# Two more feature tiles of one feed-forward half by seven half-size products, and more low parts made by adding DMAs

## The chip, the cores and the metric

One core of a Trainium2 chip runs the whole program. The metric is device microseconds of one execution, the median of the runs shown; a profiled execution is taken beside them. Engines are named as the profile names them: PE does the matrix products, ACT and DVE the elementwise work, POOL the small powers and the issue of DMAs that add, SP the issue of loads.

## The reference, cut to what matters

Two layers over 256 context and 256 latent tokens of width 1024. Each layer is a feed-forward half, a token mixer, and a second feed-forward half:

```
def swiglu(x, w_in, w_out):
    gate, up = jnp.split(x @ w_in, 2, axis=-1)
    return (jax.nn.silu(gate) * up) @ w_out

h  = h  + 0.5 * g1  * swiglu(modulate(rms_norm(h,  norm), sh1,  sc1),  ffn1_w_in, ffn1_w_out)
hc = hc + 0.5 * cg1 * swiglu(modulate(rms_norm(hc, norm), csh1, csc1), ffn1_w_in, ffn1_w_out)
# ... mixer, then the same again with norm_ffn2, sh2, sc2, g2, ffn2_w_in, ffn2_w_out
```

`w_in` is 1024 x 5632 (2816 gate and 2816 up columns), `w_out` 2816 x 1024. Context and latent tokens go through the same weights. The shifts, scales and gates come from a product of `silu(c)` with a 1024 x 9216 matrix in each layer.

## The kernel before, in words

Activations lie transposed in SBUF, 128 features by 512 tokens (256 context, 256 latent) a tile. Every operand of a large product is split in two: a high part, rounded to the matrix engine's format (`whi`, `xh`, `hh`), and a low part that holds the remainder (`wlo`, `xl`, `hl`). A product is three matmuls: high with high, high weight with low activation, low weight with high activation (`mm3`, L825 to L827).

**Four feed-forward halves.** They are named (layer, half): (0,1), (0,2), (1,1), (1,2). The 2816 features are 22 tiles of 128, in groups (`GROUPS`): in (0,2) tiles 0 to 7, 8 to 14 and 15 to 21. For a group, PE first makes the gate and up products of each tile, then contracts the group's tiles with `w_out` into the eight output tiles. A plain tile takes 16 blocks of three 512-column matmuls.

**Seven products.** From tile `DIRECT[l, half]` on, a tile is made in another way: gate and up, the two token halves and the two halves of the 1024 inputs are taken as a 2 x 2 block product, which seven products of half the size give instead of eight (`fast`, `fasts`). Each of the seven is four blocks of three 256-column matmuls, 84 matmuls a tile. The factors are sums of weight blocks and sums of activations. `seven(c)` (L711) makes the weight factors of a tile out of its two raw chunks of 512 KB: A, B, C of 1024 columns each in slots of a ring of six, and D of 512 columns in a pool of its own. Each has a high part made on ACT (`hi`, L729) and a low part made on DVE (`lo`, L723). The order of the products of tile f on PE is fixed in `fasts`: 1, 5, then product 3 of the tile before, 6, 2, product 4 of the tile before, 7. Product 2 is the first that reads B:

```
P7 = {1: ("A", 0, "X", ["A11"]), 6: ("C", 1, "X", ["C"]), ..., 2: ("B", 1, "Y", ["B"])}
for n in (1, 5, -3, 6, 2, -4, 7):
```

The opening of ring slots is a chain through the steps' waits: C of tile f waits for B of f-1, A of f+1 for C of f, B of f for A of f+1. A product that is the last to read a factor gives the slot back: 5 gives back A, 7 C, 4 B.

**Low parts by DMA.** Where `SEVENTH` (for A and B of seven-product tiles) or `SOFT` (for plain chunks) says so, the low part is not made on DVE. ACT writes the negated high part into it (`negate`, L360 for a plain chunk, L772 for A or B), and a DMA issued from POOL adds the raw weights out of HBM onto it (`add_raw`, L366; `add`, L777). Which tiles are taken follows from the fraction; for B:

```
n = SEVENTH[u, l, ww]
return int((f + 1) * n) > int(f * n)
...
if soft7("b"):
    yield S("ACT", act(1024), lambda: negate("B", whole, raw(1, whole)), give={"raw": 1}, wait=[ev("s4")])
    yield S("SW", 2.7, lambda: add("B", c + 1, whole), fire=ev("B"), lag=3.0)
```

**What sets the order.** All steps are generators with a priority (`Step`, `Weave`). At build time a planner goes through them with modelled costs and writes one fixed order of instructions for each engine; of the steps that can start within 0.12 us of each other on an engine it takes the most urgent. A smaller number is more urgent. `URG` holds four of the priorities, among weights at 18 (`U_W`), evacuation of plain tiles at 12 and the modulation products at 90. On the chip each engine runs its list in order and waits on semaphores.

**Modulation products.** The shifts, scales and gates of later stages are made on DVE (`gemv`, L882, two of 1.2 us for each of the 48, 48 and 24 jobs of the halves (0,1), (0,2), (1,1)), each after a 512 KB load. `pump` lets a number of jobs in after each plain tile, each output tile and each seven-product tile: the three numbers of `RATES` for a half. `to_mixer` (L2161) holds the next stage back until all of them are done.

**Stages in the trace.** (0,1) runs to about 395 us, the first mixer to about 600, (0,2) to 986, (1,1) to about 1330, the second mixer to about 1512, (1,2) to the end. The mixer's last output tiles overlap the first part of the half behind it.

Of the kernel before, what the change touches and what calls it, by code (L numbers as in the profile page):

```python
# [29 lines left out]
KT = 8  # L30
NF = FF // 128
GROUPS = {(0, 1): (0, 8, 15, 22), (0, 2): (0, 8, 15, 22), (1, 1): (0, 8, 15, 22), (1, 2): (0, 11, 22)}
DIRECT = {(0, 1): 13, (0, 2): 10, (1, 1): 4, (1, 2): 22}
EPS = 1e-6
CH = 8
LAT = slice(256, 512)
# [18 lines left out]
def groups(l, w):  # L55

    g = GROUPS[l, w]
    return [range(a, b) for a, b in zip(g, g[1:])]


def plan():
# [3 lines left out]
    def ffn(l, w):  # L65
# [3 lines left out]
        for fs in groups(l, w):  # L69
            for f in fs:  # L70
                if f >= DIRECT[l, w]:
                    out.extend(((kind, l, w, f), CH) for kind in ("sa", "sb"))
# [319 lines left out]
class Weave:  # L392
# [62 lines left out]
    def run(self):  # L455
# [37 lines left out]

SLACK = {"PE": 0.12, "ACT": 0.12, "DVE": 0.12, "POOL": 0.0, "DMA": 0.0, "SW": 0.0}
U_W, U_MAIN, U_EVAC, U_GEMV = 18, 50, 12, 90
URG = {'seven': 17.3, 'evac7': -5.8, 'sums': (50.8, 54.3, 50.1), 'last': 3.6}
RATES = ((8.61, 1.92, 8.82), (2.29, 5.11, 4.25), (0.59, 2.29, 1.25))
N_POOL, N_VECTOR = 6, 12
SEVENTH = {('b', 0, 1): 0, ('a', 0, 1): 0, ('b', 0, 2): 0, ('a', 0, 2): 1, ('b', 1, 1): 0, ('a', 1, 1): 0}
SOFT = {('fi', 0, 1): 0,  # L500
        ('fo', 0, 1): 0,
        ('fi', 0, 2): 0,
        ('fo', 0, 2): 0,
        ('fi', 1, 1): 0.8,
# [44 lines left out]
def emit(tc, xT, cc, wmod, wst, cols_d, cst_d, nab, gates, wm0, ccol, out, layers=L):  # L549
# [3 lines left out]
    with es:  # L553
# [25 lines left out]
        def ot():  # L579
            return op_.tile([128, 512], F32, name="o")  # L580
# [3 lines left out]
        def S(*a, **k):  # L584
            return Step(*a, **k)

        def act(n, ap=0):
            return 0.1 + 0.00083 * n + (0.0, 0.05, 0.19)[ap]
# [8 lines left out]
        def dve(n):  # L597
            return 0.06 + 0.00105 * n
# [12 lines left out]
        def half(s):  # L611
            return slice(s * 256, (s + 1) * 256)
# [98 lines left out]
        def seven(c):  # L711
# [7 lines left out]
            def raw(i, h):  # L719
                return g["ab"[i]][:, h]  # L720

            def tt(o, x0, x1, op):
                V.tensor_tensor(o, x0, x1, op)  # L723

            def ev(*e):
                return ("s7", l, ww, f) + e
# [7 lines left out]
            run = next(r for r in groups(l, ww) if f in r)  # L734
            begins, ends = f == max(run[0], DIRECT[l, ww]), f == run[-1]
            whole = slice(0, 1024)
# [4 lines left out]
            def first():  # L741
# [13 lines left out]
                if soft7("a"):  # L755
                    yield S("ACT", act(512), lambda: negate("A", a, raw(0, a)), fire=ev("nA"))
                    w.spawn(URG["seven"], a11(), w.at[ev("nA")])
                else:
# [3 lines left out]
                yield S("DVE", dve(512), lambda: tt(g["x"][:, b], raw(0, b), raw(0, a), OP.subtract), fire=ev("s2"))  # L762
                w.spawn(URG["seven"], third(), w.at[ev("s2")])
                w.spawn(URG["seven"], fourth(), w.at[ev("s2")])

            def soft7(u):

                n = SEVENTH[u, l, ww]
                return int((f + 1) * n) > int(f * n)

            def negate(u, h, src):
                A.activation(g[u][1][:, h], src, AF.Copy, scale=-1.0)  # L772
# [6 lines left out]
            def a11():  # L779
                yield S("SW", 1.4, lambda: add("A", c, a), fire=ev("A11"), lag=3.0)  # L780

            def third():
                def open_c():
                    g["C"] = W.unit()
                    hi("C", whole, g["x"])
                yield S("ACT", act(1024), open_c, take={"ring": 1}, wait=[] if begins else [other(-1, "openB")],
                        fire=ev("openC"))
                yield S("DVE", dve(1024), lambda: lo("C", whole, g["x"]), wait=[ev("s4")], give={"sx": 1},
                        fire=ev("C"))
# [11 lines left out]
            def second():  # L801
# [7 lines left out]
                if soft7("b"):  # L809
# [5 lines left out]
                        fire=ev("B"))  # L815
            w.spawn(URG["seven"], first())
            w.spawn(URG["seven"], second())

# [24 lines left out]
        def open_ffn():  # L843
            st, ph["start"] = ph["st"], _ = ExitStack(), ExitStack()
            which = ((0, 1), (0, 2), (1, 1), (1, 2))[ph.get("n", 0)]
            GF, some = max(map(len, groups(*which))), DIRECT[which] < NF
            ng = 2 if some else 6
# [183 lines left out]
        def ffn(l, ww, p, streams, nxt, rates, start):  # L1031
# [63 lines left out]

            us = dict(zip(((0, 1), (0, 2), (1, 1)), URG["sums"])).get((l, ww))

# [69 lines left out]
            def seeded():  # L1167

                def go():
                    u = S7[l, ww, DIRECT[l, ww]]["A"][0]  # L1170
                    yb.append(ot())
                    PE.matmul(yb[0][:, qa], u[:, :128], XH[:, KT - 1, half(0)], start=True, stop=True)
                yield S("PE", 0.11, go, take={"o": 1}, give={"o": 1}, wait=[("s7", l, ww, DIRECT[l, ww], "openA")])

# [33 lines left out]
            def fasts(f, run):  # L1208
                prev = f - 1 if f > max(run[0], DIRECT[l, ww]) else None
                for n in (1, 5, -3, 6, 2, -4, 7):  # L1210
# [954 lines left out]
        def main():  # L2165
            want(0, (2, 4, 3, 5, 7, 6))
            open_ffn()
            startup()
            yield from ffn(0, 1, 0, (0, 1), (0, 3), RATES[0], True)
            yield from to_mixer()  # L2170
# [3 lines left out]
            open_ffn()  # L2174
            yield from ffn(0, 2, 2, (0, 1), (1, 0), RATES[1], False)
            yield from to_mixer()
            want(1, (5, 7, 6))
            open_ffn()
            yield from ffn(1, 1, 3, (0, 1), (1, 3), RATES[2], False)
            yield from to_mixer()  # L2180
# [34 lines left out]
```

## Time and profile before

| | |
|---|---|
| median of 3 runs | 1701.85 us (1701.08 to 1703.96) |
| profiled execution, its own time | 1702.62 us |
| its span | 1700.8 us |
| PE busy | 1673.5 us, 98% |
| DVE busy | 1380.7 us, 81% |
| ACT busy | 880.4 us, 52% |
| POOL busy | 168.6 us, 10% |
| mean granted clock of PE | 0.997 |

The span runs from the first to the last instruction that the profiler saw; the time of the execution is 1.8 us more. A busy PE is not PE at its peak, since matmuls overlap: the distance between the starts of two matmuls tells its pace.

### The profile page before, as it was taken

To read this page: it belongs to the slowest core of one execution; us is meant where nothing else is said; L and a number is where in the kernel's file an instruction comes from. 1 tells how busy PE (TensorE), PEld (TensorE's weight loads), DVE (VectorE), ACT (ScalarE), POOL (GpSimd) and SP (SyncE) were. 2 spreads that over 40 slices of the span, in tenths; PEclk is the share of its full clock that TensorE was granted. 3 is DMA by queue.
4 is the path that set the end of the run, shared out by engine and by line. 5 is a ranking of instruction groups with operands and counts; after the bars stand their busy time and mean duration, and the time that the engine had idled before them with its cause. 6 is when DMAs were issued, how large, how long until landed. Compare 5 with 4: busy or idle time off the path is not lost.

```text
span 1700.8 us, 28038 instructions
## 1 busy us (share of the span) xinstructions
PE 1673.5 (98%) x10843; PEld 1455.8 (86%) x10843; DVE 1380.7 (81%) x2349; ACT 880.4 (52%) x1507; POOL 168.6 (10%) x157
## 2 busy tenths in 40 slices
PE   7999999999999999999999999999999999999999
PEld 4688888989767688888989899899898977699999
DVE  6987898997778779888989879588597878889664
ACT  4433244544768544234546465456455477765342
POOL 1201001011111110010010110200201212010000
PEclk9999999999999999999999999999999999999999
DMA  8558658373211124695786753955837323166552
GB/s 304 183 160 248 207 171 221 119 221 98 89 60 56 51 86 151 222 254 141 222 207 179 217 135 116 257 158 176 218 125 235 108 84 96 65 229 240 180 183 95
DMA packets 85273, 279.23 MB, mean 164 GB/s; under 512 B 10386, under 2 KB 13714, under 8 KB 84756
## 3 DMA queue, kind: packets, MB, share of 16 engines
q1 hardware_dynamic: 73620, 251.23, 44.8%
q0 software_dynamic: 11520, 26.22, 8.7%
q8 instruction: 85, 1.39, 0.3%
q14 instruction: 48, 0.39, 0.1%
HBM read 263.78 MB, written 1.05 MB: 156 GB/s over the span
## 4 chain that ended last, share of the span: by engine, by line
PE 88%; DVE 7%; ACT 2%; issue 2%; DMA 0%; SPq 0%; POOL 0%; POOLq 0%; ACTq 0%; DVEq 0%
PE mm L825 18%; PE mm L827 18%; PE mm L826 18%; PE mm L1193 4%; PE mm L1195 4%; PE mm L1194 4%; PE tr L1194 2%; PE tr L1193 2%; PE tr L1195 2%; PE sc L1704 1%; PE o L1757 1%; PE o L1195 1%; PE o L1194 1%; PE o L1193 1%; PE tr L1680 1%
## 5 line engine op out<-in xcount | busy, mean ns | idle before, releaser
L825 PE MATMUL mm<-xh,whi 128*128 128x512 f32 (+2 forms) x1098 | 380.8, 347 | 3.1 <-ACT xh L975 1.9
L826 PE MATMUL mm<-xl,whi 128*128 128x512 f32 (+2 forms) x1098 | 365.9, 333 | 3.8 <-DVE xl L976 2.7
L827 PE MATMUL mm<-xh,wlo 128*128 128x512 f32 (+2 forms) x1098 | 365.0, 332 | 0.0
L349 ACT CAST whi<-wraw 128x1024 fp32r<-128x1024 f32 (+1 forms) x238 | 248.4, 1044 | 212.3 <-PE mm L826 173.1
L882 DVE SCALAR_TENSOR_TENSOR junk<-graw,silc 128x1024 f32<-128x1024 f32 x256 | 315.9, 1234 | 24.9 <-DMA graw<-in_wmod_dram 22.3
L355 DVE TENSOR_TENSOR wlo<-wraw,whi 128x1024 fp32r<-128x1024 f32 (+2 forms) x213 | 260.2, 1223 | 69.0 <-ACT whi L349 67.5
L827 PE MATMUL mm<-hh,wlo 128*128 128x512 f32 (+1 forms) x724 | 260.8, 360 | 0.0
L826 PE MATMUL mm<-hl,whi 128*128 128x512 f32 (+1 forms) x724 | 258.5, 357 | 0.0
L825 PE MATMUL mm<-hh,whi 128*128 128x512 f32 (+1 forms) x724 | 258.4, 357 | 0.0
L825 PEld LDWEIGHTS mm<-xh,whi 128*128 128x128 f32 x1098 | 208.0, 189 | 35.2 <-issue 10.3
L826 PEld LDWEIGHTS mm<-xl,whi 128*128 128x128 f32 x1098 | 208.4, 190 | 30.0 <-issue 5.3
L827 PEld LDWEIGHTS mm<-xh,wlo 128*128 128x128 f32 x1098 | 208.0, 189 | 22.2 <-DVE wlo L355 0.4
L826 PEld LDWEIGHTS mm<-hl,whi 128*128 128x128 f32 x724 | 136.1, 188 | 23.4
L825 PEld LDWEIGHTS mm<-hh,whi 128*128 128x128 f32 x724 | 136.1, 188 | 21.5
L827 PEld LDWEIGHTS mm<-hh,wlo 128*128 128x128 f32 x724 | 136.0, 188 | 21.3
L723 DVE TENSOR_TENSOR wlo<-wraw,whi 128x512 fp32r<-128x512 f32 (+1 forms) x105 | 92.4, 886 | 35.6 <-ACT whi L729 35.2
L729 ACT CAST whi<-wraw 128x512 fp32r<-128x512 f32 (+1 forms) x117 | 88.9, 763 | 49.9 <-PE mm L826 32.1
L1024 ACT ACTIVATE h<-mm,mod 128x256 f32<-128x256 f32 x96 | 40.4, 472 | 128.2 <-PE mm L827 93.8
L1195 PE MATMUL mm<-t7h,wlo 128*128 128x256 f32 x312 | 88.1, 282 | 0.0
L1194 PE MATMUL mm<-t7l,whi 128*128 128x256 f32 x312 | 87.9, 282 | 0.0
L1028 POOL DMA_DIRECT2D x<-h x48 | 41.9, 873 | 463.3 <-ACT h L1024 358.1
L1193 PE MATMUL mm<-t7h,whi 128*128 128x256 f32 x312 | 87.7, 281 | 0.0
(312 smaller groups left out, 3530.8 us busy)
## 6 DMA issues: line engine op xcount, KB each, us to landing
wraw<-in_wst_dram SPq DMA_DIRECT2D x308, 512.0 KB, 3.7
graw<-in_wmod_dram SPq DMA_DIRECT2D x137, 512.0 KB, 4.6
x<-h POOLq DMA_DIRECT2D x48, 256.0 KB, 5.7
wlo<-in_wst_dram POOLq DMA_DIRECT2D x20, 512.0 KB, 9.1
graw<-in_wm_dram SPq DMA_DIRECT2D x7, 512.0 KB, 7.1
silc<-in_cc_dram SPq DMA_DIRECT2D x3, 1024.0 KB, 7.0
wlo<-in_wst_dram POOLq DMA_DIRECT2D x12, 256.0 KB, 4.5
x<-in_xT_dram SPq DMA_DIRECT2D x8, 256.0 KB, 4.3
```

Of the source, the lines that this page charges most:

```text
L349: self.nc.scalar.copy(hi[:, :n], self.raws[i][:, :n])
L355: eng.tensor_tensor(lo[:, :n], self.raws.pop(i)[:, :n], hi[:, :n].bitcast(F32), OP.subtract)
L723: V.tensor_tensor(o, x0, x1, op)
L729: A.copy(g[u][0][:, h], src)
L825: PE.matmul(o, wh[:, :m], h, start=start, stop=False)
L826: PE.matmul(o, wh[:, :m], lo, start=False, stop=False)
L827: PE.matmul(o, wl[:, :m], h, start=False, stop=stop)
L882: V.scalar_tensor_tensor(ph["junk"], g["r"], 1.0, ph["sc"][:, s, :], OP.mult, OP.mult, accum_out=mod[l, c][:, s, j:j + 1])
L1028: yield S("SW", 1.4, lambda: G.dma_start(x[:, dt, :], g["t"], accum_op=OP.add), lag=3.0, give={"h": 1})
L1193: PE.matmul(o, wh, xh, start=n in (1, 5) and k == 0, stop=False, **on)
L1194: PE.matmul(o, wh, xl, start=False, stop=False, **on)
L1195: PE.matmul(o, wl, xh, start=False, stop=k == 3, **on)
```

## The change

Numbers that the planner reads are changed, and no function. `DIRECT` of (0,2) goes from 10 to 8, so tiles 8 to 21, 14 of them, are made by seven products, where 10 to 21 were. Of the low parts of A in (0,2) half are made by adding DMAs, where all were; of B 0.34, where none were. In (0,1) half of the low parts of A and a quarter of the plain `w_out` chunks (from chunk 12 on) are made by adding DMAs, where none were. `URG` and `RATES` get other values.

```
-DIRECT = {(0, 1): 13, (0, 2): 10, (1, 1): 4, (1, 2): 22}
+DIRECT = {(0, 1): 13, (0, 2): 8, (1, 1): 4, (1, 2): 22}
...
-URG = {'seven': 17.3, 'evac7': -5.8, 'sums': (50.8, 54.3, 50.1), 'last': 3.6}
-RATES = ((8.61, 1.92, 8.82), (2.29, 5.11, 4.25), (0.59, 2.29, 1.25))
+URG = {'seven': 14, 'evac7': -6.6, 'sums': (39.8, 22.4, 49.5), 'last': 3.6}
+RATES = ((2.5, 0.61, 32.34), (19.02, 20.23, 51.94), (0.3, 2.64, 5.69))
...
-SEVENTH = {('b', 0, 1): 0, ('a', 0, 1): 0, ('b', 0, 2): 0, ('a', 0, 2): 1, ('b', 1, 1): 0, ('a', 1, 1): 0}
+SEVENTH = {('b', 0, 1): 0,
+           ('a', 0, 1): 0.5,
+           ('b', 0, 2): 0.34,
+           ('a', 0, 2): 0.5,
+           ('b', 1, 1): 0,
+           ('a', 1, 1): 0}
 SOFT = {('fi', 0, 1): 0,
-        ('fo', 0, 1): 0,
+        ('fo', 0, 1): 0.25,
         ('fi', 0, 2): 0,
```

## Rows read from the trace of the kernel before

**Rows 1.** The page, part 1: busy time (share of the span) and instructions.

```profile
PE 1673.5 (98%) x10843; PEld 1455.8 (86%) x10843; DVE 1380.7 (81%) x2349; ACT 880.4 (52%) x1507; POOL 168.6 (10%) x157
```

**Rows 2.** Stretches: length, busy us of PE, PEld, DVE, ACT, POOL; PEclk, DMA share, GB/s.

```profile
66.00:395.00 329.00, 329.00 (x1810) 283.32 (x1810) 294.59 (x473) 137.20 (x224) 22.65 (x21) 1.00 0.64 191
645.00:986.00 341.00, 341.00 (x2033) 301.12 (x2032) 298.70 (x472) 159.19 (x267) 33.73 (x37) 1.00 0.69 200
```

**Rows 3.** Timeline of PE: start, us, line, operation; tile 8 begins, seven products begin.

```profile
764.67 0.39 PE L825 MATMUL mm<-xh,whi 128*128 128x512 f32 x1
...
787.15 0.28 PE L1172 MATMUL o<-xh,whi 128*128 128x256 f32 x1
```

**Rows 4.** Timeline of PE: product 2 of tiles 16, 17; between, product 1 of 17.

```profile
889.52 0.28 PE L1195 MATMUL o<-xh,wlo 128*128 128x256 f32 x1
...
893.54 0.28 PE L1193 MATMUL mm<-xh,whi 128*128 128x256 f32 x1
...
899.40 0.28 PE L1195 MATMUL o<-xh,wlo 128*128 128x256 f32 x1
```

**Rows 5.** Timeline of ACT: high part of B of tile 17, [idle before <-releaser].

```profile
892.18 1.05 ACT L729 CAST whi<-wraw 128x1024 fp32r<-128x1024 f32 x1 [0.91 <-PE mm L1194]
893.14 0.61 ACT L1235 CAST hh<-h 128x512 fp32r<-128x512 f32 x1
```

**Rows 6.** Timelines of ACT and POOL: one negation and its 512 KB adding DMA.

```profile
963.63 1.06 ACT L360 ACTIVATE wlo<-wraw 128x1024 fp32r<-128x1024 f32 x1
...
965.09 0.88 POOL L366 DMA_DIRECT2D wlo<-in_wst_dram  x1 [0.73 <-ACT wlo L360]
```

**Rows 7.** Line L366, 512 KB adds: all 20, then the three of 960:980.

```profile
DMA to landing us min/median/max: 7.0/9.1/12.3
...
DMA to landing us min/median/max: 7.0/7.0/7.7
```

**Rows 8.** Line L777, 256 KB adds of A: the four of 880:925.

```profile
DMA to landing us min/median/max: 4.0/4.1/6.8
```

**Rows 9.** Stretches, columns as in rows 2.

```profile
880.00:925.00 45.00, 45.00 (x384) 45.00 (x383) 43.09 (x74) 29.37 (x55) 3.48 (x4) 1.00 0.62 162
1062.00:1074.00 12.00, 12.00 (x97) 11.72 (x96) 10.10 (x19) 6.86 (x12) 1.73 (x2) 1.00 0.95 269
```

**Rows 10.** Two neighbouring stretches of the start, columns as in rows 2.

```profile
55.00:58.40 3.40, 0.80 (x4) 0.21 (x2) 3.40 (x7) 2.04 (x4) 0.70 (x1) 0.99 0.66 235
58.40:61.60 3.20, 3.20 (x8) 2.52 (x9) 3.13 (x5) 0.83 (x2) 0.00 (x0) 0.50 0.05 19
```

**Rows 11.** DVE groups in 645:986: shapes, count, busy us, mean ns, idle before.

```profile
L355 DVE TENSOR_TENSOR wlo<-wraw,whi 128x1024 fp32r<-128x1024 f32 x36 | 44.5, 1237 | 7.2 <-ACT whi L349 7.1
L723 DVE TENSOR_TENSOR sx<-wraw 128x512 f32<-128x512 f32 x24 | 16.5, 688 | 0.3
...
L1231 DVE TENSOR_TENSOR h<-sg,h 128x256 f32<-128x256 f32 x12 | 5.0, 420 | 0.4 <-ACT sg L1228 0.4
```

**Rows 12.** Timelines: end of the last modulation job; first product of (1,1).

```profile
970.03 0.17 DVE L896 TENSOR_TENSOR mod<-mod,cols 128x16 f32<-128x16 f32 x1
...
986.06 0.28 PE L825 MATMUL mm<-xh,whi 128*128 128x256 f32 x1
```

**Rows 13.** Timelines: B's high part and product 2 of tiles 14 and 15.

```profile
820.57 1.05 ACT L729 CAST whi<-wraw 128x1024 fp32r<-128x1024 f32 x1
...
830.34 0.28 PE L1195 MATMUL o<-xh,wlo 128*128 128x256 f32 x1
...
865.17 1.05 ACT L729 CAST whi<-wraw 128x1024 fp32r<-128x1024 f32 x1 [1.87 <-PE mm L826]
...
880.97 0.28 PE L1195 MATMUL o<-xh,wlo 128*128 128x256 f32 x1
```

**Rows 14.** Timelines: first output chunk of (0,1)'s last group, cast and first use.

```profile
344.86 1.05 ACT L349 CAST whi<-wraw 128x1024 fp32r<-128x1024 f32 x1 [0.40 <-PE mm L1194]
...
359.40 0.40 PE L827 MATMUL mm<-hh,wlo 128*128 128x512 f32 x1
```

## The prediction

> **What bounds the kernel.** I read the page's busy shares first, then the table of stretches, then the timelines of PE, ACT, DVE and POOL around the seven-product tiles of (0,2), and last the adding DMAs by line. PE is busy 98% of the span [rows 1], and in the two stretches that the change touches, 66 to 395 us for (0,1) and 645 to 986 us for (0,2), it is busy for the whole length at a granted clock of 1.00 [rows 2]. The pace agrees: between the start of tile 8 and the start of the seven products lie two plain tiles, 96 matmuls in 787.15 - 764.67 = 22.48 us, 0.234 us each with no gap [rows 3]. So in (0,1) and (0,2) the time is PE's column count, and nothing that only relieves DVE or ACT shortens it. DVE is the next: 298.7 of 341 us in (0,2) and 294.6 of 329 us in (0,1) [rows 2]. A gain must come out of fewer matmul columns, and a loss out of any factor that reaches PE late.
>
> **Two tiles fewer by the plain way.** A plain tile costs 22.48 / 2 = 11.24 us [rows 3]. A seven-product tile in the steady part of a group costs the distance of product 2 of tile 16 to product 2 of tile 17, 899.40 - 889.52 = 9.88 us [rows 4]. Two tiles change kind: 2 x (9.88 - 11.24) = -2.7 us. They are tiles 8 and 9, so that group two becomes like group three, all seven tiles of one kind; group three runs without a gap today, so I charge no new seam.
>
> **DVE's part of it.** A plain tile has two subtractions of 1024 and two of 512 columns, 2 x 1.24 + 2 x 0.69 = 3.9 us. A seven-product tile has two of 1024, eight of 512 (one of them A's low part) and four of 256: 2.5 + 5.5 + 1.7 = 9.7 us [rows 11]. Two tiles add 11.6 us. Twelve A parts went by DMA and seven will: +3.4 us. Five B parts leave DVE: 5 x 1.24 = -6.2 us. Net +8.8 us in a stretch that has 42 us of idle DVE, mostly in slivers. What gives way are the modulation jobs, the least urgent work. The last one ends at 970.2 us, and PE needs it at 986.06, when (1,1) begins [rows 12]: 15.9 us of cover, less the 2.7 us that PE gains. If all 8.8 us came out one for one as delay, 4.4 us would be left. I charge 0; with that cover gone each further microsecond of DVE is one of PE.
>
> **B's low part by DMA.** The rule with 0.34 takes tiles 8, 11, 14, 17 and 20. Tile 17 stands in the trace. B's high part is cast at 892.18, after ACT had waited 0.91 us for PE to give a ring slot back, and ends at 893.23 [rows 5]. The first matmul that reads B's low part starts at 899.40 [rows 4]. That leaves 6.2 us, and the lead can't grow with earlier work, because the slot, not ACT or DVE, sets it: the six openings of two tiles lie between B of tile 15 and B of tile 17, and B of 15 is given back by product 4, one product (1.4 us) before tile 17 begins. Today DVE fills the gap with 1.2 us of work. In its place come: the cast of `hh`, more urgent, to 893.75 [rows 5]; the negation, 1.06 us; 0.40 us from its end to the start of the DMA on POOL (964.69 to 965.09) [rows 6]; and the landing of a 512 KB adding DMA. For the landing the nearest rows are the 20 of line L366, 7.0 to 12.3 us with a median of 9.1 [rows 7], and the 256 KB adds of A in this very stretch, 4.0 to 6.8 us [rows 8]. The stretch moves data in 0.62 of its time, against 0.95 where the pair of slowest adds was under way [rows 9], and the three adds in 960 to 980 took 7.0 to 7.7 us [rows 7]. I take 7.0: the low part is there at 893.75 + 1.06 + 0.40 + 7.0 = 902.2 us, 2.8 us late. PE's list has nothing to put in the gap, since the order of the products is fixed and in-order. Bounds: with 4.1 us it is on time (0), with 12.3 us it is 8.1 us late.
>
> Tiles 11, 17 and 20 are of this steady kind: third, fourth or sixth in their groups. Each stall stands for itself, because the next lead is again counted from PE's own release: 3 x 2.8 = 8.4 us. Tile 14 is last in its group and has more: its cast ends at 821.62 and product 2 needs the low part at 830.34, 8.7 us, against 1.06 + 0.40 + 7.0 = 8.5: 0 (with 9.1 us 1.9 late). Tile 8 will open its group as tile 15 does now, with 880.97 - 866.22 = 14.7 us [rows 13]: 0 at any landing in the rows.
>
> The Trainium skill has a rule that speaks against this stall: "DMA: Bandwidth & Descriptors", section "Anatomy of one DMA", fits a DMA issued from POOL with 2.0 us plus its bytes over 436 GB/s. For 512 KB that is an estimate of 3.2 us; by it the low part of tile 17 would be there at 898.4 us, before PE wants it, and the sum would be -2.7 us alone. This case's trace does not agree: no add of that size landed under 7.0 us, and none of half the size in this stretch under 4.0 [rows 7, 8].
>
> **The clock.** Near 57 us PE stood for 2.6 us of 3.4, and its granted clock was then 0.50 for 3.2 us, which is 1.2 in place of 2.4 GHz [rows 10]: half of 3.2, 1.6 us, lost. A stall of 2.8 us is of that size, and whether it is followed by such a spell I can't tell from one row. Bounds 0 and 3 x 1.6; I take one in three, +1.6 us.
>
> **The rest at nothing.** Half of A's low parts in (0,1), tiles 13, 15, 17, 19, 21: A is opened a whole tile and more before its product, so adds of 4 to 7 us [rows 8] lie in front of more than 10 us of other products; 0. A quarter of the output chunks of (0,1): the tightest is the first of the last group, cast to 345.91 and wanted at 359.40, 13.5 us [rows 14], against 1.06 + 0.40 + 9.1 = 10.6; 0, and 0.3 us at the longest landing. These edits take 5 x 0.69 + 5 x 1.24 = 9.7 us off DVE in (0,1), where PE has no gap to close: 0 as well. On POOL's queue the new adds stand among the 256 KB adds of output tiles and delay none that PE waits for. `URG`: 17.3 to 14 stays between 12 and 18, -6.6 stays the first, and the sums pass nothing that runs beside them but keep ahead of 90; the order by priority is the same. `RATES`: in (0,1) fewer jobs are let in early, but their two load buffers and the idle time of DVE hold them back more than the letting in does; in (0,2) and (1,1) jobs enter some tiles sooner and still fill only what others leave. 0, with perhaps 1 us either way in the mixers, whose order the planner weaves anew.
>
> **The sum.** -2.7 + 8.4 + 1.6 = +7.3 us on the profiled execution's own time, 1702.62 us: 1709.9. That execution is 0.8 us above the median of the runs, so I predict 1709.1, rounded to 1709 us, 0.4% slower.
>
> **Rivals.**
> *The adds land in time, not slower.* If a 512 KB add lands within 4.2 us of its issue (899.40 - 895.21), nothing stalls: 1701.85 - 2.7 = 1699.2 us. For it speak the adds of 256 KB in this stretch, median 4.1 [rows 8]; against it that twice the bytes would have to take no longer, and the floor of 7.0 [rows 7]. The point of decision is that 4.2 us. Chance 0.25. This is the case that the rule of the Trainium skill above would give.
> *The adds take their median.* Negation frees the raw buffer sooner, the next 512 KB load sets out beside the add, and the landing is 9.1 us: 3 x 4.9 + 1.9 = 16.6 us, three spells of the clock 4.8: 1701.85 - 2.7 + 21.4 = 1720.5 us. For it speaks that the same holds at line L366; against it the lighter DMA traffic [rows 9]. Chance 0.15.
> *DVE becomes the bound at the end of (0,2).* The modulation jobs end after PE's last contraction and `to_mixer` holds PE. It decides above 13.2 us of delay (15.9 - 2.7) [rows 12]; twice the 8.8 us would cost 4.4 us, without late adds 1703.6. Chance 0.04.
> *Something else gets shorter.* Without stalls, and with a mixer that the planner happens to weave 1 us or more better: 1698 us or less. Nothing in the trace speaks for it beyond the mixers' gaps. Chance 0.06.
>
> **How the numbers follow.** The forecast has 0.50. A measurement of this kernel can tell about 0.2% from no change, 3.4 us: 1698.4 to 1705.3. The forecast's own range is 1704 to 1715 (landings of 6 to 8.3 us, none or all of the spells); nearly all of it and all of the median rival are slower: 0.67. In time, and most of the DVE rival: same, 0.26. The rest faster, 0.07. The range reaches down to the case without a stall, 1699, and up into the median rival, 1717.
>
> **What would show it.** Right: idle time of PE before a low-part matmul of product 2 (line L1195, `o<-xh,wlo`) released by the adding DMA of line L777, three times, 2 to 4 us each, in the groups of tiles 8 to 14 and 15 to 21; 512 KB adds on L777 of about 7 us; 9.9 us a tile elsewhere; no gap in (0,1). The prediction is wrong if those adds land within 4.2 us, if B opens more than 8 us before product 2, or if PE waits at the start of (1,1) for DVE.

## The result, and the profile after

The kernel after takes 1719.11 us (median of 4 runs, 1718.08 to 1720.90), the kernel before 1701.80 in the same comparison: a ratio of 1.0099, 95% interval 1.0085 to 1.0114. That is 17.3 us slower; 7.3 were predicted, and the range ended 2.1 us below the measurement. The profiled execution took 1720.90 us (span 1719.1), against 1702.62 (span 1700.8): 18.3 us between them.

Two lines of the page, part 1 and part 6 (count, KB each, median us from issue to landing). PE has 72 more matmul records but only 5 us more of busy time for an 18 us longer span. Of the 30 adds of 512 KB in the second line only five are B's; the others are those of L366, 20 of which were there before [rows 7]:

```profile
PE 1678.5 (98%) x10915; PEld 1464.9 (85%) x10915; DVE 1377.6 (80%) x2360; ACT 895.3 (52%) x1531; POOL 175.9 (10%) x166
...
wlo<-in_wst_dram POOLq DMA_DIRECT2D x30, 512.0 KB, 8.8
```

All lines of the seven-product code stand 5 lower than before (L1195 is L1200, L777 is L782). PE's timeline around product 2, which reads B's low part (`o<-xh,wlo`); in brackets the idle time before the instruction and what ended it:

```profile
798.57 0.28 PE L1199 MATMUL o<-xl,whi 128*128 128x256 f32 x1
803.18 0.58 PE L1200 MATMUL o<-xh,wlo 128*128 128x256 f32 x1 [4.33 <-DMA wlo<-in_wst_dram]
...
815.55 0.28 PE L1200 MATMUL o<-xh,wlo 128*128 128x256 f32 x1
...
825.43 0.28 PE L1200 MATMUL o<-xh,wlo 128*128 128x256 f32 x1
...
909.33 0.58 PE L1200 MATMUL o<-xh,wlo 128*128 128x256 f32 x1 [4.80 <-DMA wlo<-in_wst_dram]
...
944.34 0.39 PE L1200 MATMUL o<-xh,wlo 128*128 128x256 f32 x1 [2.87 <-DMA wlo<-in_wst_dram]
```

Three waits, on tiles 11, 17 and 20, and none on 8 and 14; between undisturbed tiles the pace is 825.43 - 815.55 = 9.88 us, as for tiles 16 and 17 before [rows 4]. The adding DMAs by line (17 on L782, with A's) say the same from the other side, who waited for them:

```profile
who waited for it (us, times):
  PEld o L1200: 12.6, 3
  PE o L1200: 12.0, 3
...
DMA to landing us min/median/max: 3.8/6.8/9.2
```

The stretches (length, then busy us of PE, PEld, DVE, ACT, POOL; PEclk, DMA share, GB/s): the whole of (0,2), the first wait and the two stretches behind it, what lies behind the second and third wait, and the end of (0,1):

```profile
645.00:986.00 341.00, 328.99 (x1995) 294.19 (x1994) 293.85 (x469) 158.56 (x267) 28.71 (x31) 0.97 0.67 194
798.84:803.18 4.34, 0.01 (x1) 0.00 (x1) 4.30 (x8) 0.70 (x2) 0.00 (x0) 0.81 0.99 250
803.18:806.00 2.82, 2.82 (x13) 2.82 (x14) 0.82 (x2) 0.28 (x1) 0.00 (x0) 0.50 0.89 243
806.00:808.30 2.30, 2.30 (x13) 2.30 (x13) 0.02 (x1) 0.34 (x2) 0.00 (x0) 0.50 0.49 191
...
909.30:914.00 4.70, 4.67 (x22) 4.67 (x23) 0.00 (x0) 0.38 (x1) 0.00 (x0) 0.50 0.48 181
...
944.30:948.00 3.70, 3.66 (x19) 3.66 (x20) 1.21 (x3) 0.38 (x1) 0.00 (x0) 0.58 0.78 241
...
375.00:425.00 50.00, 48.14 (x340) 45.39 (x340) 39.17 (x75) 20.06 (x36) 9.50 (x8) 0.97 0.34 108
```

Each wait is followed by a stretch at half clock, 1.2 GHz: (1 - 0.50) x (2.82 + 2.30) + (1 - 0.50) x 4.70 + (1 - 0.58) x 3.70 = 6.5 us. In the kernel before, PE was busy to 395.34 us, the end of (0,1); now a gap stands there. The stretch of 375 to 425 us in the kernel before:

```profile
375.00:425.00 50.00, 49.05 (x352) 45.76 (x351) 40.25 (x78) 21.84 (x39) 9.95 (x8) 1.00 0.36 113
```

That is 49.05 - 48.14 = 0.9 us of idle time and 0.03 x 48.14 = 1.4 of clock. The gap itself, in the profile after, on PE and on DVE:

```profile
394.73 0.61 PE L961 MATMUL sc<-cst,acc 128*128 128x1 f32 x4 [1.48 <-DVE acc L933]
...
391.39 1.22 DVE L887 SCALAR_TENSOR_TENSOR junk<-graw,silc 128x1024 f32<-128x1024 f32 x1
...
392.65 0.59 DVE L901 TENSOR_TENSOR mod<-mod,cols 128x16 f32<-128x16 f32 x1
393.16 0.47 DVE L1014 SCALAR_TENSOR_TENSOR x<-mm,mod,x 128x256 f32<-128x256 f32 x1
394.25 0.43 DVE L933 TENSOR_TENSOR acc<-acc,nsq 128x256 f32<-128x256 f32 x1 [0.61 <-ACT nsq L929]
```

PE waits for the last sum of the norm (`acc`), and in DVE's list a modulation product and the end of its job stand right ahead of the step (`x`) that this sum needs. In the kernel before, the last modulation product ended at 390.41 us, 3.8 us ahead of that step. So it is DVE's order that changed there; no add is waited for.

The sum by these rows: waits 4.33 + 4.80 + 2.87 = 12.0, clock 6.5, end of (0,1) 2.4, two tiles -2.7: 18.2 us, against 18.3 between the two profiled executions. So nearly all of the loss has a place. That the sum closes to 0.1 us is chance: from 30 to 66 us the granted clock was 0.86 in the profiled execution of before and 1.00 in that of after, PE's work of (0,1) ended at 395.34 and at 393.25 us, and about as much, 2 us, lies in differences that these rows don't name. The experiments ask whether the loss would go away with its cause.

### The profile page after: what moved, and what is told of

Its sections match the earlier page's. It is cut to its first block, busy times and chain, and to the rows that moved or that the text cites. A ratio compares the mean times of both kernels' runs of the same rounds, so it can differ in the third digit from the quotient of the medians.

```text
span 1719.1 us, 28222 instructions
## 1 busy us (share of the span) xinstructions
PE 1678.5 (98%) x10915; PEld 1464.9 (85%) x10915; DVE 1377.6 (80%) x2360; ACT 895.3 (52%) x1531; POOL 175.9 (10%) x166
## 4 chain that ended last, share of the span: by engine, by line
PE 81%; DVE 7%; issue 5%; DMA 3%; ACT 2%; POOL 1%; SPq 0%; POOLq 0%; ACTq 0%; DVEq 0%
PE mm L830 16%; PE mm L831 16%; PE mm L832 16%; PE mm L1198 4%; PE mm L1199 4%; PE mm L1200 4%; PE tr L1199 2%; PE tr L1198 2%; PE tr L1200 2%; DMA wlo<-in_wst_dram 2%; PE sc L1709 1%; PE o L1762 1%; PE o L1200 1%; PE tr L1685 1%; PE o L1199 1%
## 5 line engine op out<-in xcount | busy, mean ns | idle before, releaser
L830 PE MATMUL mm<-xh,whi 128*128 128x512 f32 (+2 forms) x1066 | 367.8, 345 | 3.8 <-ACT xh L980 2.6
L831 PE MATMUL mm<-xl,whi 128*128 128x512 f32 (+2 forms) x1066 | 352.7, 331 | 4.1 <-DVE xl L981 3.0
L832 PE MATMUL mm<-xh,wlo 128*128 128x512 f32 (+2 forms) x1066 | 351.8, 330 | 0.0
L355 DVE TENSOR_TENSOR wlo<-wraw,whi 128x1024 fp32r<-128x1024 f32 (+2 forms) x204 | 249.0, 1222 | 71.7 <-ACT whi L349 70.3
L830 PEld LDWEIGHTS mm<-xh,whi 128*128 128x128 f32 x1066 | 201.7, 189 | 34.8 <-issue 9.9
L831 PEld LDWEIGHTS mm<-xl,whi 128*128 128x128 f32 x1066 | 202.0, 189 | 28.7 <-issue 5.3
L832 PEld LDWEIGHTS mm<-xh,wlo 128*128 128x128 f32 x1066 | 201.7, 189 | 20.3
L1198 PE MATMUL mm<-xh,whi 128*128 128x256 f32 x328 | 93.6, 285 | 0.0
L1199 PE MATMUL mm<-xl,whi 128*128 128x256 f32 x328 | 93.4, 285 | 0.0
L1200 PE MATMUL mm<-xh,wlo 128*128 128x256 f32 x328 | 93.4, 285 | 0.0
```

The source lines that it names most:

```text
L355: eng.tensor_tensor(lo[:, :n], self.raws.pop(i)[:, :n], hi[:, :n].bitcast(F32), OP.subtract)
L830: PE.matmul(o, wh[:, :m], h, start=start, stop=False)
L831: PE.matmul(o, wh[:, :m], lo, start=False, stop=False)
L832: PE.matmul(o, wl[:, :m], h, start=False, stop=stop)
L1198: PE.matmul(o, wh, xh, start=n in (1, 5) and k == 0, stop=False, **on)
L1199: PE.matmul(o, wh, xl, start=False, stop=False, **on)
```

## The experiments: the late adds

The theory on record was that the late adds of B are all of the loss. The rival was that DVE, which gets two more tiles to prepare, or the other new numbers, would have cost the time anyway. Times are medians; ratios are to the kernel before, with 95% intervals. The planner writes a new order for each kernel whose steps or modelled costs change, so waits can come and go in other places too.

**No B adds.** The changed kernel with one number set back:

```diff
-           ('b', 0, 2): 0.34,
+           ('b', 0, 2): 0,
```

> The changed kernel with B's low parts on DVE again. Late adds (the three adding DMAs of B and the clock spells behind them are the whole loss): no gap of PE over 0.5 us in tiles 8 to 21, and 1699 to 1701 us, which is 2.7 us less than before, up to 1 us either way for the stage ends. Rival (two more seven-product tiles, or the other new numbers, overload DVE): still above 1710 us, with gaps elsewhere in that stretch.

Measured: 1715.24 us, 1.0080 (1.0066 to 1.0093). Only 4 of 17 us came back, so the theory in its simple form falls. The three waits are gone, and others stand in their place: 2.06 us at product 5 of a tile at 804.5, 3.70 and 1.36 at the end of (0,2) in front of the norm sums, and 2.53 at product 5 in (1,1). The first two:

```profile
804.51 0.38 PE L1200 MATMUL tr<-t7h,wlo 128*128 128x256 f32 x1 [2.06 <-DVE wlo L728]
...
990.39 0.37 PE L961 MATMUL sc<-cst,acc 128*128 128x1 f32 x1 [3.70 <-POOL acc L933]
```

The second ends with POOL, but followed further back its chain goes through a modulation product on DVE (986.55) and, ahead of that, 9.70 us until the product's load had landed.

**B adds alone.** The kernel before with `('b', 0, 2): 0.34`, so adds on tiles 11, 14, 17 and 20 of its twelve:

> The kernel before with the 0.34 for B alone, which takes tiles 11, 14, 17 and 20 of the twelve. Late adds: tiles 17 and 20 stall as in the changed kernel, 4.5 us and a clock spell of 2.1 us each; tile 11 is now second in its group with a lead of 8.7 us and is about 1.5 us late: 13 to 17 us above before, 1715 to 1719 us. Rival (the B adds hurt only together with the two more tiles): within 3 us of before.

Measured: 1713.38 us, 1.0068 (1.0054 to 1.0082), 11.6 us slower by the ratio. That is 1.6 below the expected range. PE waits for these adds 0.62, 3.83 and 2.18 us (tiles 11, 17, 20); behind the second the clock was 0.54 for 3.7 us, behind the other two 1.00. The late adds cost by themselves, without the two tiles.

**Adds only where the lead is long.** The changed kernel with B's adds on tiles 8 and 15, the first of their groups:

```diff
             def soft7(u):
 
+                if (u, l, ww) == ("b", 0, 2):
+                    return f in (8, 15)
                 n = SEVENTH[u, l, ww]
```

> The changed kernel with B's low parts by DMA on tiles 8 and 15 alone, the first of each group, where B is cast 13 to 15 us ahead of product 2. Late adds (it is the lead and not the DMA that costs): both land 8 to 9 us after their issue and PE doesn't wait; the time of the run without B adds within 1 us. Rival (a 512 KB add in this stretch costs in itself, by holding up the loads): about 4 us or more above that run, with gaps at other products.

Measured: 1721.53 us, 1.0117 (1.0103 to 1.0131). Nobody waits for an add, so the lead of an opening tile is long enough; but the kernel is the slowest so far, with 3.49 and 1.35 us at the end of (0,2), 5.31 at the start of (1,1) and 2.53 at its product 5. The first two end with POOL's work on the norm, the third with a step of ACT (`sg`), the last with a low part from DVE. At 6.3 us over the run without B's adds this is the rival's range. But three of the four waits were in that run as well, the end of (0,2) again behind a modulation load, of 10.0 us; new is the third, in front of which DVE was busy 37.3 of 42.5 us with modulation products among its steps. Whether the two adds held up the loads or the new order did it is not shown.

**The wait filled.** The changed kernel with 37 matmuls of 256 columns (4.4 us) ahead of product 2 on tiles 11, 17 and 20. Nothing uses what they make; PE is kept busy where it stood idle.

```diff
...
                 for n in (1, 5, -3, 6, 2, -4, 7):
+                    if n == 2 and (l, ww) == (0, 2) and f in (11, 17, 20):
+                        yield S("PE", 4.4, lambda: filler(f), take={"sc": 1}, give={"sc": 1})
```

> The changed kernel with 37 matmuls of 256 columns put in front of product 2 of tiles 11, 17 and 20; their result is used by nothing. They fill 4.4 us in which PE stood. If the clock spells are a cost of their own (6.4 us of the 18): granted clock 1.00 through the stretch, next to no wait left, and 1712 to 1715 us. Rival (no own cost of the clock; PE catches nothing up): the same time as the changed kernel within 2 us, or more by what the filler takes.

Measured: 1716.11 us, 1.0084 (1.0070 to 1.0097): 3.0 us less than the changed kernel (no run of the one reaches into the other's), though the filler is 3 x 4.4 - 12.0 = 1.2 us longer than the waits. It is in neither range, 1.1 us above the first. The clock stays at 1.00 in all three places, and one wait of 0.48 us for an add is left. So by the medians about 4 us of the 6.5 are the price of having stood still.

**DVE relieved.** In the changed kernel each modulation product of (0,2) reads 64 columns and not 1024, 0.22 us of DVE where it took 1.22; the order stays.

```diff
             def dot(s):
-                V.scalar_tensor_tensor(ph["junk"], g["r"], 1.0, ph["sc"][:, s, :], OP.mult, OP.mult,
+                n = 64 if ph["n"] == 2 else 1024
+                V.scalar_tensor_tensor(ph["junk"][:, :n], g["r"][:, :n], 1.0, ph["sc"][:, s, :n], OP.mult, OP.mult,
                                        accum_out=mod[l, c][:, s, j:j + 1])
```

> The changed kernel, order untouched, with each modulation product of stage (0,2) reading 64 columns where it read 1024 (some 1.1 us less of DVE for each of 96 products; the loads stay whole). The modulation values of that stage are then not the reference's. If the late adds cost by themselves, whatever DVE has to do: the three gaps at product 2 of tiles 11, 17 and 20 stay (12.5 us with 6.4 us of slower clock behind them), 1714 to 1719 us. If the adds are late only because DVE is behind: gaps under 1 us, 1698 to 1703.

Measured: 1720.42 us, 1.0105 (1.0090 to 1.0120). The adding DMAs of this run by line:

```profile
who waited for it (us, times):
  PEld o L1201: 13.0, 3
  PE o L1201: 12.4, 3
...
DMA to landing us min/median/max: 3.7/6.2/9.2
```

The same three waits, 12.4 us in place of 12.0; the time is 1.4 us above the range for this case. A DVE that was behind is not why the adds are late.

**The add reads SBUF.** B's add takes the raw chunk from the buffer in which it lies already, where it read HBM a second time. The buffer is given back when the add has landed.

```diff
-                    yield S("ACT", act(1024), lambda: negate("B", whole, raw(1, whole)), give={"raw": 1},
-                            wait=[ev("s4")])
-                    yield S("SW", 2.7, lambda: add("B", c + 1, whole), fire=ev("B"), lag=3.0)
+                    yield S("ACT", act(1024), lambda: negate("B", whole, raw(1, whole)), wait=[ev("s4")])
+                    yield S("SW", 2.7, lambda: G.dma_start(g["B"][1][:, whole], raw(1, whole), accum_op=OP.add),
+                            fire=ev("B"), lag=3.0, give={"raw": 1})
```

> The changed kernel with B's adding DMA reading the raw tile that lies in SBUF already, where it read HBM a second time (the raw buffer is held until the add lands, so later weight loads may start later). If the way from HBM makes the add slow: landing 3 to 5 us after issue where 8.8 was the median, gaps at product 2 under 2 us, and with fewer loads delayed 1708 to 1713. If the adding transfer itself, or the other transfers beside it, set the pace: landing 7 to 10 us as before, gaps of 4 to 5 us again, 1717 to 1723.

Measured: 1714.08 us, 1.0073 (1.0058 to 1.0088). Its DMA issues from 740 to 960 us (count, KB each, median us to landing):

```profile
wraw<-in_wst_dram SPq DMA_DIRECT2D x40, 512.0 KB, 4.6
...
wlo<-wraw POOLq DMA_DIRECT2D x5, 512.0 KB, 5.4
```

and the same view of the changed kernel:

```profile
wraw<-in_wst_dram SPq DMA_DIRECT2D x38, 512.0 KB, 3.8
...
wlo<-in_wst_dram POOLq DMA_DIRECT2D x5, 512.0 KB, 8.0
```

The same add lands 2.6 us sooner from SBUF (median), though the loads of the stage land later (4.6 after 3.8). The waits at product 2 shrink to 1.45 and 2.64 us and one below 1, and 5.0 us come back. Waits of 2.05 and 2.07 us at product 5 appear, and one of 1.36 at 837.4. Landing, waits and time all lie between the two expected ranges, nearer to the first. What flew beside the adds changed as well: over the flights of tiles 11, 17 and 20 the DMA share was 0.75, 0.79 and 0.76, where it had been 0.88, 0.89 and 0.99. So how much of the 2.6 us is the source's is not shown.

**Product 2 last.** The changed kernel with `for n in (1, 5, -3, 6, -4, 7, 2)`. The line serves the seven-product tiles of all halves, so the new order holds in (0,1) and (1,1) too, and not in (0,2) alone.

> The changed kernel with product 2 as the last of each tile's seven in (0,2), two products (2 x 1.42 us) later than where it stood. If the adds are late by what the gaps show (4.5, 5.0 and 3.0 us): gaps of 1.7, 2.1 and 0.2 us remain and their clock spells shorten, but DVE loses the time in which it caught up: 1708 to 1713. If the wait moves with the product (the add's start hangs on the order too): gaps as before, 1717 to 1721.

Measured: 1715.36 us, 1.0081 (1.0066 to 1.0096), in neither range. The waits for adds shrink to 0.22 us on tile 17 and 1.37 on tile 20, but not by the gaps: 1.7, 2.1 and 0.2 had been expected on 11, 17 and 20. The new order brings waits of its own (1.09, 1.10 and 1.38 at product 5, 1.22 and smaller ones at product 7).

## The experiments: what stands behind the late adds

**Two tiles and nothing else.** The kernel before with `(0, 2): 8` in `DIRECT`.

> The kernel before with 14 feature tiles of seven products in (0,2) and nothing else of the change (A's low part by an adding DMA on every one of them, as before; B's on DVE). DVE gets the two tiles' work, +10.2 us by the rows of before, none of it taken off. Theory 1, only the late adds cost, DVE's 15.9 us of cover holds: 1699 to 1702 us. Theory 2, DVE has no such room and what it gets comes out as a wait at the end of (0,2), where modulation jobs stand ahead of the norm: 1706 to 1712. Theory 3, the loss that stayed without B's adds is from the other new numbers (order and rates): 1699 to 1702 here, and over 1707 in the next two.

**The changed kernel with A's adds on all 14 tiles and no B adds** (`('a', 0, 2): 1`, `('b', 0, 2): 0`).

> The changed kernel with A's low part by an adding DMA on all 14 tiles and B's never: DVE's list is that of the run above (+10.2 us against before, where the run without B's adds had +15.0), in the new numbers' order. Theory 1: 1699 to 1702. Theory 2: 1706 to 1712, as the run above within 2. Theory 3: over 1707 while the run above is under 1702.

**The changed kernel without the two tiles and without B adds** (`(0, 2): 10`, `('b', 0, 2): 0`).

> The changed kernel with 12 feature tiles of seven products in (0,2) as before, and no adding DMA for B; A's adds are still halved there (+4.8 us of DVE against before), and all other new numbers stand. Theory 1: 1700 to 1703. Theory 2: 1703 to 1707. Theory 3: over 1707.

Measured: 1706.19 us, 1.0025 (1.0014 to 1.0036); 1708.14, 1.0041 (1.0028 to 1.0053); 1706.82, 1.0032 (1.0020 to 1.0043). Each of the three gives DVE more to do (11.6 - 2 x 0.69 = 10.2 us in the first two; 6 x 0.69 = 4.1 in the third, where the expectation's 4.8 was a slip), and each is slower, in the second theory's ranges, though not in the place it named: nothing waits at the end of (0,2). It is a wait of 2.0 us at product 5, two of them in the first two kernels and one in the third. The second and third have the gap at the end of (0,1) as well (1.25 and 1.40 us of waiting). PE's timeline in the first:

```profile
803.05 0.39 PE L1195 MATMUL tr<-t7h,wlo 128*128 128x256 f32 x1 [2.03 <-DVE wlo L723]
```

and DVE's, in its program order:

```profile
797.98 0.42 DVE L1231 TENSOR_TENSOR h<-sg,mm 128x256 f32<-128x256 f32 x1 [0.61 <-PE mm L1195]
798.32 0.69 DVE L723 TENSOR_TENSOR sx<-wraw 128x512 f32<-128x512 f32 x1
799.04 0.69 DVE L723 TENSOR_TENSOR wraw<-wraw 128x512 f32<-128x512 f32 x1
799.65 0.68 DVE L1259 TENSOR_TENSOR hl<-h,hh 128x512 fp32r<-128x512 f32 x1
800.25 0.41 DVE L1231 TENSOR_TENSOR h<-h,mm 128x256 f32<-128x256 f32 x1
800.58 1.22 DVE L723 TENSOR_TENSOR wlo<-wraw,whi 128x1024 fp32r<-128x1024 f32 x1
801.72 0.68 DVE L723 TENSOR_TENSOR sx<-wraw 128x512 f32<-128x512 f32 x1
802.32 0.68 DVE L723 TENSOR_TENSOR wlo<-wraw,whi 128x512 fp32r<-128x512 f32 x1
```

The last line makes the low part that product 5 waits for. Once PE's product has released its first line (797.98), DVE works without a pause, and `hl`, `h` and B's low part, 801.72 - 799.65 = 2.07 us, stand ahead of it: about the length of the wait. DVE had itself stood idle 0.61 us for that product of PE; its order counts here, not its load alone.

**One late add.** The second of these kernels with a B add on tile 17 alone.

> The second run of this call (A's adds on all 14 tiles) with one adding DMA for B, on tile 17: one late add alone, where all five were. DVE has 1.2 us less than there. Late adds with their clock spell: 5 to 8 us over the second run, with one gap of 4 to 5 us at product 2 of tile 17 and a stretch at half clock behind it. If DVE's load were all that counts: equal to the second run or up to 1.5 us below it.

Measured: 1709.74 us, 1.0051 (1.0035 to 1.0066), 1.6 us over the run without it, in neither range. The wait for the add is there, 3.71 us at tile 17, but the wait at product 5 of the tile behind it is gone: while PE stands, DVE makes up its arrears. The two costs don't add.

**Short modulation products, no B adds.** The run without B's adds (`('b', 0, 2): 0`), with DVE relieved as above.

> The kernel of the run without B's adds (+13.3 us against before), order untouched, with the same short modulation products in (0,2). If DVE's load made its waits (product 5 at 802 and 1058, the end of (0,2) at 986): they vanish and 1698 to 1701 remain, 2.7 under before, the worth of two tiles. If DVE's order or a load that lands late made them: the wait at 986 stays, 1706 to 1713. If the other new numbers cost by themselves: over 1704 without those waits.

Measured: 1714.71 us, 1.0079 (1.0063 to 1.0096): nothing gained, and 1.7 above the range for a wait that stays (by the rows DVE has 11.6 + 3.4 = 15.0 us more than before; the expectation's 13.3 was a slip). Its stretches, (0,2) and what follows, and two lines of DVE's timeline, ahead of the wait at product 5 and in the gap at the end:

```profile
645.00:986.00 341.00, 338.61 (x2104) 302.57 (x2103) 215.83 (x489) 161.28 (x274) 26.55 (x31) 1.00 0.67 197
986.00:1000.00 14.00, 9.76 (x63) 9.68 (x64) 13.59 (x39) 7.55 (x16) 1.67 (x2) 0.76 0.66 186
```

```profile
800.35 0.42 DVE L1237 TENSOR_TENSOR h<-sg,mm 128x256 f32<-128x256 f32 x1 [1.01 <-PE mm L1201]
...
985.63 0.23 DVE L888 SCALAR_TENSOR_TENSOR junk<-graw,silc 128x64 f32<-128x64 f32 x1 [1.52 <-DMA graw<-in_wmod_dram]
```

DVE is busy 216 of 341 us and PE waits all the same, because the order was written for the long products. At the end of (0,2) a modulation product stands ahead of the norm, and DVE sits in front of it until its load has landed. At product 5 the wait stays too, 2.07 us at 805.46, though DVE had stood idle for 1.01 us at 800.35: the low part stands behind a step that PE itself releases.

**The same with an order for short products.** The planner is told their true length:

```diff
-                   yield S("DVE", 1.14, lambda: dot(s), wait=[("graw", l, c, j), ("silc", ph["n"], s)],
+                   yield S("DVE", 0.25 if ph["n"] == 2 else 1.14, lambda: dot(s), wait=[("graw", l, c, j), ("silc", ph["n"], s)],
```

> The run without B's adds and with short modulation products in (0,2) (1714.7 us), where now the planner also reckons with their short time (0.25 us where it stood at 1.14), so that DVE's order is drawn up for a DVE with room. The modulation values of (0,2) are not the reference's. If the waits came of an order made for a full DVE: the modulation products all stand ahead of the end of (0,2), the waits at product 5 and at the end go, 1699 to 1703. If they come of the two tiles' own chain, whatever DVE has to do: 1708 to 1715.

Measured: 1701.61 us, 1.0000 (0.9991 to 1.0009). Stretches (0,2) and the end of (0,1):

```profile
645.00:986.00 341.00, 340.28 (x2117) 304.47 (x2116) 222.48 (x502) 162.36 (x277) 23.78 (x28) 1.00 0.66 197
375.00:425.00 50.00, 48.55 (x339) 45.63 (x338) 39.96 (x77) 19.84 (x36) 9.70 (x8) 0.97 0.36 109
```

PE is full again in (0,2), but for two gaps of 0.36 us. What is left is the gap in (0,1), about 2 us, and it is paid for by the two tiles' 2.7.

**That order with products of full length**, with the new numbers and with those of before (14 tiles, A's adds on all):

> The run without B's adds with the order drawn up for short modulation products in (0,2), whose products are of full length again: all work of the stage is there. If a better order was all that was lacking: 1700 to 1704, as with the short products. If DVE is truly full: the products of 1.2 us that now stand earlier push DVE's subtractions back and PE waits in the feature tiles of (0,2), 1710 to 1725.

> The kernel before with 14 tiles of seven products in (0,2), A's adds on all of them, and the order drawn up for short modulation products there, the products being of full length. Order alone: 1698 to 1702, the two tiles' 2.7 us gained or nearly. DVE truly full: 1706 to 1720.

Measured: 1727.44 us, 1.0150 (1.0135 to 1.0165), and 1723.55, 1.0122 (1.0105 to 1.0139). Both are above their ranges. Stretch (0,2) of the first, and its longest wait, at the contraction of the first group:

```profile
645.00:986.00 341.00, 321.59 (x1969) 284.99 (x1968) 304.09 (x481) 148.42 (x257) 20.09 (x23) 0.98 0.64 187
...
736.17 0.79 PE L830 MATMUL mm<-hh,whi 128*128 128x512 f32 x1 [9.49 <-ACT hh L1069]
```

The chain ahead of that wait is modulation products on DVE and, between them, two modulation loads that DVE stands in front of (4.97 and 4.22 us). So four cases without B adds: long products in the order for long ones 1715.2, short in that order 1714.7, short in their own order 1701.6, long in the order for short ones 1727.4. Neither the order nor the load alone does it: with DVE's true load PE is kept waiting in each of the orders built here. That no order would do is not shown.

**Another order.** Two tiles and nothing else, with `'seven': 0` in `URG`.

> The kernel before with 14 tiles of seven products in (0,2), all else as before (1706.2 us, two waits of 2.2 us at product 5), and one number of the order changed: the seven-product chains' urgency 0, not 17.3. DVE's work is the same. If the waits hang on the place of S1's low part in DVE's order: in the new order no tile of (0,2) has s1, s2 and S1's low part behind B's low part in the same way, waits gone or under 1 us there, 1698 to 1703 (other stages are re-ordered too and may add). If DVE's amount of work sets them: 1704 to 1709 in this order as well.

Measured: 1715.30 us, 1.0080 (1.0067 to 1.0093). Missed: the waits at product 5 of (0,2) are gone, but the sums of activations come late where the seven products begin, five waits of 0.46 to 1.54 us at 779 to 785, and again in (1,1).

**Parts alone, on the kernel before.** A's adds in (0,2) halved (`('a', 0, 2): 0.5`), and the new adds of (0,1) (`('a', 0, 1): 0.5`, `('fo', 0, 1): 0.25`):

> The kernel before, with A's adding DMA in (0,2) on every second of its 12 seven-product tiles and not on all: 6 subtractions of 0.69 us more for DVE, and the last of them in another order. If it is that which cost e8_rest its 5 us: one wait of 2.2 us at product 5 of a tile in the second group with its clock spell, 1704 to 1706. If DVE's cover takes it: 1701 to 1703.

> The kernel before with only the new adds of stage (0,1): A's on every second seven-product tile, a quarter of the output weights' low parts. I charged this nothing. If nothing: 1701 to 1702.5. If the end of (0,1), where the runs with these adds had 0.7 to 2.6 us more of PE's waits at 375 to 425 us, is theirs: 1702.5 to 1704.5.

Measured: 1704.66 us, 1.0018 (1.0010 to 1.0027), with one wait of 2.02 us at product 5; and 1705.37, 1.0019 (1.0011 to 1.0028), 0.9 above its range. The end of (0,1) in the second:

```profile
375.00:425.00 50.00, 48.41 (x343) 45.76 (x342) 39.76 (x77) 20.46 (x36) 9.70 (x8) 0.97 0.34 111
```

It is the gap of the changed kernel, 0.6 us of idle time and 1.5 of clock; a wait of 1.25 us for DVE at 946.3, in (0,2), comes with it. With the new `URG` and `RATES` alone the built program has the instructions of before in the same order on all five engines, buffer numbers apart; so it was not run. The changed kernel, built with the `URG` and `RATES` of before, likewise keeps its own instructions and order.

## Why the prediction went wrong

**Right.** Two tiles at -2.7 us: the pace of 9.88 us stands, and the kernel with a relieved DVE and its own order ends, within its interval, where -2.7 and the gap in (0,1) put it. The path of B: on tile 11 ACT casts the high part, then `hh`, then the negation,

```profile
791.38 1.05 ACT L734 CAST whi<-wraw 128x1024 fp32r<-128x1024 f32 x1 [0.92 <-PE mm L1199]
792.33 0.61 ACT L1240 CAST hh<-h 128x512 fp32r<-128x512 f32 x1
792.85 1.06 ACT L777 ACTIVATE wlo<-wraw 128x1024 fp32r<-128x1024 f32 x1
...
794.31 0.89 POOL L782 DMA_DIRECT2D wlo<-in_wst_dram  x1 [15.40 <-DVE h L1236]
```

and the add is issued 794.31 - 793.91 = 0.40 us after the negation's end (the last line puts POOL's idle time down to a step of DVE that ended 0.3 us later, but all 12 adds on L782 in (0,2) are issued 0.40 us after their negation, whatever stands there), step for step as [rows 5, 6] gave it. Tiles 11, 17 and 20 wait, 8 and 14 don't. `URG` and `RATES` at nothing. The waits, then, were foreseen as to place and mechanism; three terms of the sum were too small, by 3.6 us (the waits), 4.9 (the clock) and 2.4 (the end of (0,1)).

**The step that failed first: "For the landing ... I take 7.0".** The five adds landed 8.0, 8.8, 7.5, 9.2 and 7.8 us after their issue. The waits are 4.33, 4.80 and 2.87 us where 2.8 each were put: 12.0 in place of 8.4. The reason for 7.0 was that the stretch moved data in 0.62 of its time [rows 9]. That is a mean, and no 512 KB add was in it. Over the flights of the five adds the share was 0.98, 0.88, 0.90, 0.89 and 0.99, their own packets included. In the kernel before, the three adds of line L366 whose flights had shares of 0.70 to 0.81 are those that landed in 7.0 to 7.7 us; the 17 others, with shares of 0.85 and more, took 7.8 to 12.3. So rows in the same company would have said about 8 or more. A share read at the place itself in the trace of before would not: from 895.2 to 904.2 us, where the add of tile 17 was to fly, it was 0.69.

The rival that took the median of line L366 gave 1720.5 us, 1.4 from the measurement; it had 0.15. In part that was luck: it put 16.6 us of waits where 12.0 came, 4.8 of clock where 6.5 came, and no gap in (0,1).

**"I take one in three, +1.6 us".** This is the larger error. In the profiled execution all three waits are followed by half clock, 2.6, 2.4 and 1.6 us lost, 6.5 in all. The price from the row of the start [rows 10], 1.6, was low, and the count was a guess at what one row couldn't tell. It isn't the same in every kernel: of the three waits for adds on the kernel before, one was followed by slow clock.

**"DVE's part ... I charge 0".** This step failed too, but the changed kernel doesn't show it: with PE standing still for 12 us, DVE gets time. Where the add reads SBUF and PE stands for 4.8 us, waits at product 5 appear, with the same work on DVE. Take the adds away and give the kernel before two tiles alone, and the charge shows: 4.6 us slower by the medians (4.3 by the ratio) where 2.7 should have been gained. The cover was read at one place, the last modulation product at 970.2 us [rows 12], as if DVE's work could be pushed from tile to tile to the end of the stage. But in the feature tiles of group three DVE was busy 43.09 of 45 us [rows 9], and there each tile has its own time by which a low part must be there. The 42 us of idle DVE lie elsewhere. The bound "if all 8.8 us came out one for one" stood on the same cover, so it left the cost at nothing as well.

**"No gap in (0,1)", charged 0.** The new adds there cost 3.2 us by themselves (1.9 to 4.8), some 2 of them at this place, and 2.4 in the profile after. The working looked at when the adds land and at what DVE is spared. It left out that a list of DVE without these low parts is another list, in which a modulation product comes to stand ahead of the last sum of the norm.

The Trainium skill's page "DMA: Bandwidth & Descriptors", section "Anatomy of one DMA", fits a DMA issued from POOL with 2.0 us plus its bytes over 436 GB/s, from which comes an estimate of 3.2 us for 512 KB. No run here agrees with it: 7.5 to 9.2 us from HBM and a median of 5.4 from SBUF, both of them adding transfers. The same page of the Trainium skill, section "Queues, rings and completion order", says that a DMA engine takes turns between the queues that have work for it; that B's adds land late beside SP's loads (shares of 0.88 to 0.99 over their flights) agrees with it, but no run here shows the turns.

What stays open: why an add from HBM takes 2.6 us longer than one from SBUF, and whether some order exists in which 14 tiles fit DVE. One more buffer for raw chunks, or one more ring slot, was not tried. No version beat the kernel before.

## What to carry to other kernels

When work moves from a compute engine to a DMA, price the transfer by rows taken while the same other transfers are in flight, not by a stage's mean DMA share, and put a price on the clock that may fall behind each wait of PE. When an in-order engine is busy 96% in a stretch, don't count its idle time elsewhere in the stage as cover for work that has a due time in each tile: look at what stands ahead of that work in the engine's list. Work taken off an engine changes its list too. And a change that loses in two places may show only one of them: here the late adds hid the waits for DVE, and undoing the adds gave back 4 of 17 us.

## What the runs showed of the hardware

A 512 KB add onto SBUF landed in 5.4 us (median of five) when it read SBUF and in 8.0 when it read HBM, in the same stretch of the same stage but with other loads beside it, where a plain load of that size from HBM, issued on SP, took 3.8 to 4.6 (medians). And the clock fell after some short waits as well, not after all. After waits of 2.05 and 2.07 us in the kernel whose add reads SBUF, and of 2.02 us in the kernel before with A's adds halved, the granted clock stayed at 1.00; in the kernel with two tiles and nothing else PE waited 2.0 us up to 915.8 us, and the clock from 916 to 919 was 0.56. What decides it is not shown.

```profile
916.00:919.00 3.00, 3.00 (x17) 3.00 (x17) 3.00 (x5) 2.29 (x6) 0.00 (x0) 0.56 0.43 150
```
